# An MLP in two passes of half the tokens, its up projection by seven products of quarters

## The chip, the cores and the metric

The kernel runs on one core of a Trainium2 chip. The metric is the device time of one execution in microseconds (us). A core has TensorE for matrix products (PE in the profile), VectorE (DVE), ScalarE (ACT) and GpSimd (POOL) for the elementwise work, and DMA queues; SP is the engine that issues most DMAs, POOL issues the rest. Each engine takes its instructions in the order of its own program and waits on semaphores for the others. Matrix products go into PSUM, everything else lies in SBUF.

## The reference

The reference is one decoder layer on 1032 tokens (1024 of a prompt and 8 single steps of decoding), width 1024, with RMSNorm, one input projection, a pooling mixer and an RWKV-7 mixer, an output projection and an MLP. The change touches the last three lines:

```
mix = concatenate([pool_out, rwkv_out]) @ w_out
x = x + mix
h2 = rmsnorm(x, norm2_g)
x = x + square(relu(h2 @ w_up)) @ w_down        # w_up 1024x4096, w_down 4096x1024
y = rmsnorm(x, norm_f_g)
```

All of it is float32. The kernel splits each float32 operand into a high part h, rounded to the fp32r type, and a rest l, and computes a product as h·h + h·l + l·h: three matmuls.

## The kernel before

Features lie on the 128 partitions, tokens on the free axis: an activation of 1024 features is 8 tiles (index k or m), and the tokens are cut into blocks of 512, 260 and 260 columns (`BLK`). The residual x is held in two tiles, half 0 of 512 and half 1 of 520 tokens.

A weight tile is 128 x 512. `weights` (L147 to L167) loads it through POOL's queue into one of 4 buffers `wr`, ScalarE rounds it into `wh` (L92, the helper `act`) and VectorE subtracts, `wl` (L165); there are 6 pairs `wh`, `wl`. `gemm` (L169) issues the three matmuls for each of its input tiles (L175).

After the mixers comes the output projection (`mx`): first of half 0, then of half 1 (L938 to L949), where each of 8 m has two blocks of 21 matmuls of 260 columns. A block goes into one of two PSUM buffers (`ps_d`), and VectorE adds it to x (L880), which gives the buffer back. The x of half 1 comes by `load_x1` (L853). Then `norm2` makes h2 (h on ScalarE, l on VectorE, L913) and the root mean square.

The MLP: `up(f, w, b)` (L922) computes one of 32 feature tiles f for a token block: 24 matmuls (8 k times 3); VectorE applies relu and the scale (L931), squares (L932) and, after ScalarE's rounding, makes the rest `ul` (L934). `down(g, m, b, w)` takes four finished f (one g) for one m: 12 matmuls, and VectorE adds to x (L971). The loop L974 to L982 alternates four f of up with one g of down. Each weight is loaded once and serves the three blocks. The last g goes block by block with the final RMSNorm (L1001 to L1021), which VectorE applies (L993).

The order on each engine comes from a scheduler that takes the program text, buffers and dependencies and writes one list for each engine before the kernel runs; the buffers that a tile waits for are fixed with it.

## Time and profile before

| what | value |
| --- | --- |
| three runs | 1361.23, 1358.73, 1359.34 us; median 1359.34 |
| profiled execution | 1360.81 us, its span 1359.0 |
| mean granted clock of TensorE | 0.992 of full speed |
| TensorE busy | 1303.5 us, 96% of the span |
| VectorE busy | 823.5 us, 61% |
| ScalarE busy | 574.7 us, 42% |
| MLP, from first to last up and down product | about 614 to 1347 us |

Times below are from the profiled execution, in us from the start of its span, unless a duration is meant. A busy TensorE need not be at its peak: matmuls are pipelined, so the time that one costs is the distance from its start to the next one's, shorter than the duration shown. The same holds on VectorE. PEclk is the granted clock as a share of 2.4 GHz; 0.50 is 1.2 GHz.

### The profile page before, as it was taken

Reading aid. Unit: us, or ns where it says so; the run is one execution under the profiler, and the core shown is the slowest. Engines: PE = TensorE matmul, PEld = TensorE weight load, DVE = VectorE, ACT = ScalarE, POOL = GpSimd, SP = SyncE. Lnnn points to the kernel's source line nnn. Section 1 sums busy time; section 2 is a strip of 40 time slices with the busy share of each in tenths; the row PEclk is TensorE's granted clock in tenths of the full one; section 3 lists DMA queues with packets and bytes.
Section 4 is the critical chain, followed back from the end, with each engine's and each line's share of the span. In section 5 each row is a group of like instructions: output and inputs, shape, how many; then the busy total and the mean of one; then the engine's idle time right before and its main releaser. Section 6 shows DMA issues by size and latency. Waiting matters only on the chain.

```text
span 1359.0 us, 24513 instructions
## 1 busy us (share of the span) xinstructions
PE 1303.5 (96%) x9844; PEld 1154.2 (85%) x9844; DVE 823.5 (61%) x1790; ACT 574.7 (42%) x1417; POOL 156.9 (12%) x306
## 2 busy tenths in 40 slices
PE   5999999899999989899999999999999999999996
PEld 5987878798777867798999999999999999999986
DVE  7887686778777756749534435445344354453457
ACT  7668677766877666626211112112111121121123
POOL 4101001210100211120100000000000000000000
PEclk9999999999999979999999999999999999999998
DMA  6323123322211452621111111111111111111103
GB/s 204 102 54 80 42 49 90 102 87 61 62 51 40 105 175 100 201 92 47 56 51 44 50 47 45 49 46 47 50 46 48 47 46 47 46 48 49 47 6 125
DMA packets 81650, 94.55 MB, mean 70 GB/s; under 512 B 52504, under 2 KB 58776, under 8 KB 81528
## 3 DMA queue, kind: packets, MB, share of 16 engines
q0 software_dynamic: 20480, 66.04, 15.2%
q1 hardware_dynamic: 59728, 25.10, 7.2%
q8 instruction: 77, 1.26, 0.4%
q10 hardware_dynamic: 1328, 1.85, 0.4%
q14 instruction: 37, 0.30, 0.1%
HBM read 79.67 MB, written 13.51 MB: 69 GB/s over the span
## 4 chain that ended last, share of the span: by engine, by line
PE 78%; ACT 9%; DVE 7%; DMA 3%; issue 2%; POOL 0%; DVEq 0%; SPq 0%; ACTq 0%; POOLq 0%
PE dn L175 26%; PE up L175 26%; PE pj L175 8%; PE mx L175 5%; ACT SV L92 2%; PE pcs L598 1%; PE sc L421 1%; PE pcs L595 1%; ACT TT L92 1%; DVE tm L515 1%; PE pcs L591 1%; PE bkt L435 1%; DMA wr<-in_w_in 1%; PE py L599 1%; DMA x<-in_xT 1%
## 5 line engine op out<-in xcount | busy, mean ns | idle before, releaser
L92 ACT ACTIVATE wh<-wr 128x512 fp32r<-128x512 f32 x230 | 143.8, 626 | 355.7 <-PE dn L175 276.2
L175 PE MATMUL up<-h2h,wl 128*128 128x260 f32 (+1 forms) x768 | 245.6, 320 | 0.0
L175 PE MATMUL up<-h2h,wh 128*128 128x260 f32 (+1 forms) x768 | 245.0, 320 | 0.5 <-DVE u L931 0.5
L175 PE MATMUL up<-h2l,wh 128*128 128x260 f32 (+1 forms) x768 | 244.8, 319 | 0.0
L175 PE MATMUL dn<-uh,wl 128*128 128x512 f32 (+1 forms) x720 | 231.0, 321 | 0.0
L175 PE MATMUL dn<-ul,wh 128*128 128x512 f32 (+1 forms) x720 | 230.6, 320 | 0.0
L175 PE MATMUL dn<-uh,wh 128*128 128x512 f32 (+1 forms) x720 | 230.3, 320 | 0.0
L971 DVE TENSOR_TENSOR x<-dn,x 128x260 f32<-128x260 f32 (+1 forms) x192 | 99.1, 516 | 189.6 <-PE dn L175 189.6
L175 PE MATMUL pj<-xh,wh 128*128 128x258 f32 (+3 forms) x576 | 172.8, 300 | 13.9 <-ACT wh L92 13.9
L165 DVE TENSOR_TENSOR wl<-wr,wh 128x512 fp32r<-128x512 f32 x230 | 156.5, 684 | 44.7 <-ACT wh L92 38.0
L175 PE MATMUL pj<-xl,wh 128*128 128x258 f32 (+3 forms) x576 | 170.8, 297 | 0.0
L175 PE MATMUL pj<-xh,wl 128*128 128x258 f32 (+3 forms) x576 | 170.6, 296 | 0.1
L175 PEld LDWEIGHTS up<-h2l,wh 128*128 128x128 f32 x768 | 144.5, 188 | 12.1 <-DVE h2l L913 0.4
L175 PEld LDWEIGHTS up<-h2h,wh 128*128 128x128 f32 x768 | 144.1, 188 | 11.7 <-DVE u L931 0.9
L175 PEld LDWEIGHTS up<-h2h,wl 128*128 128x128 f32 x768 | 144.4, 188 | 11.1
L92 ACT ACTIVATE uh<-u 128x260 fp32r<-128x260 f32 (+1 forms) x96 | 47.2, 492 | 238.5 <-DVE u L932 238.5
L175 PEld LDWEIGHTS dn<-ul,wh 128*128 128x128 f32 x720 | 135.5, 188 | 10.9 <-issue 0.2
L175 PEld LDWEIGHTS dn<-uh,wh 128*128 128x128 f32 x720 | 135.7, 188 | 10.5
L175 PEld LDWEIGHTS dn<-uh,wl 128*128 128x128 f32 x720 | 135.4, 188 | 10.6 <-issue 0.2
L175 PEld LDWEIGHTS pj<-xh,wh 128*128 128x128 f32 x576 | 110.4, 192 | 17.8 <-ACT wh L92 13.9
L931 DVE SCALAR_TENSOR_TENSOR u<-up,rs 128x260 f32<-128x260 f32 (+1 forms) x96 | 49.5, 516 | 120.8 <-PE up L175 114.3
L175 PEld LDWEIGHTS pj<-xl,wh 128*128 128x128 f32 x576 | 110.6, 192 | 2.3 <-issue 1.9
(293 smaller groups left out, 2187.6 us busy)
## 6 DMA issues: line engine op xcount, KB each, us to landing
wr<-in_w_in POOLq DMA_DIRECT2D x72, 256.0 KB, 3.1
wr<-in_w_up POOLq DMA_DIRECT2D x64, 256.0 KB, 2.9
wr<-in_w_down POOLq DMA_DIRECT2D x64, 256.0 KB, 2.9
wr<-in_w_out POOLq DMA_DIRECT2D x26, 256.0 KB, 3.2
xr<-in_xT SPq DMA_DIRECT2D x16, 256.0 KB, 3.6
mr<-mix SPq DMA_DIRECT2D x8, 260.0 KB, 3.5
x<-in_xT SPq DMA_DIRECT2D x2, 1040.0 KB, 9.4
blk<-AA SPq DMA_DIRECT2D x16, 128.0 KB, 2.8
```

The source lines that it names most:

```text
L92: A.activation(out, in_, func, bias=bias, scale=scale, **k)
L165: V.tensor_tensor(l[:, :w], raw[:, :w], f32(h[:, :w]), op=ALU.subtract)
L175: PE.matmul(ps, lhs, rhs, start=i == 0, stop=i == n - 1)
L421: PE.matmul(psc[:, c, :], BK[:, c, 2 * h:2 * h + 2, :], AR[:, c, :, h, :], start=True, stop=True)
L435: PE.transpose(pt[:, c, :], BK[:, c, 2 * h:2 * h + 2, :].rearrange("p a t -> p (a t)"), ident)
L515: V.tensor_tensor(pr[:, q], l[:, q].unsqueeze(2).to_broadcast([64, m, m, m]), r[:, q].rearrange("p k j -> p j k").unsqueeze(1).to_broadcas ...
L591: PE.matmul(pq, AR[:, c, 0, :, :], SV[:, c, :, :], start=True, stop=True)
L595: PE.matmul(pa, TT[:, g, :, :], Q, start=True, stop=True)
L598: PE.matmul(pu, BKT[:, c, :, :], SV[:, c, :, :], start=True, stop=True)
L599: PE.matmul(py[:, c, :, :], SV[:, c, :, :], RB[:, c, :, :], start=False, stop=True)
L931: V.scalar_tensor_tensor(u, ps[:, :n], 0.0, rs2[:, cs], ALU.max, ALU.mult)
L971: V.tensor_tensor(d, ps[:, :n], d, op=ALU.add)
```

## The change

The tokens are processed in two passes: half 0 (512 tokens), then half 1 (520), and within a pass a product of a pair of feature tiles (256 output features), all 1024 inputs and the half's tokens is computed as a 2 x 2 by 2 x 2 block product by Strassen's scheme in Winograd's form. Quarters of the weights: output tile f or f+1 by inputs k 0 to 3 or 4 to 7. Quarters of the activations: inputs k 0 to 3 or 4 to 7 by the first or second half of the pass's tokens.

`up_operands(half)` normalises x fully and makes the seven activation operands (`KIND`), each as h and l, 4 tiles of 128 x 256 or 260. For each k of 4 it has 4 `normed`, 4 `less` and 7 `put`, so in all 60 instructions of VectorE and 28 of ScalarE for one half. `up_pair(p)` loads four weight quarters, single-buffered, through SP's queue, makes four sums on VectorE, splits seven operands, runs seven products of 12 matmuls of 256 or 260 columns, adds them up (`plus`, seven on VectorE) and applies relu and square on ScalarE (`emit`). Generators (`downs`) put down products of an earlier group between the products of a pair. Each weight of the MLP is now loaded twice, once for each half, which is 128 more loads of 256 KB, and all of them go through SP's queue. The final norm of half 0 comes in the middle (group 7), so the last group has only the two blocks of half 1.

```diff
+NXT = 8
+NUT = 10
...
-    def weights(src, into=None):
+    def weights(src, into=None, q=GP):
...
-                GP.dma_start(raw[:, :w], src[:, o:o + w])
+                q.dma_start(raw[:, :w], src[:, o:o + w])
...
+    def split(raw):
+
+        h = wp.tile([P, 512], F32R, tag="wh", name="wh", bufs=NWH)
+        l = wp.tile([P, 512], F32R, tag="wl", name="wl", bufs=NWH)
+        act(h, raw)
+        V.tensor_tensor(l, raw, f32(h), op=ALU.subtract)
+        return h, l
...
-    h2 = [hq.tile([P, KT, T], F32R, tag=f"h2{x}", name=f"h2{x}") for x in "hl"]
+
+    KIND = ("11", "t2", "21", "t3", "t1", "22", "t4")
+    XO = [{}, {}]
     rs2 = hq.tile([P, T], F32, name="rs2")
...
     def norm2(c, n, tmp):
-        for m in range(KT):
-            x, h, g = x1s(m, c, n), h2[0][:, m, c:c + n], col(V_G2, m)
-            act(h, x, scale=g)
-            V.scalar_tensor_tensor(h2[1][:, m, c:c + n], x, g, f32(h), ALU.mult, ALU.subtract)
         ss = ps_m.tile([P, 512], F32, tag="m", name=f"ss2{c}")
         acc = tmp(f"acc2{c}")[:, :n]
         for m in range(KT):
-            square_sum(ss, m, c, n, acc, m and tmp(f"sq2_{c}_{m}")[:, :n])
+            sq = tmp(f"sq2_{c}_{m}")[:, :n] if m else acc
+            act(sq, x1s(m, c, n), AF.Square)
+            if m:
+                V.tensor_tensor(acc, acc, sq, op=ALU.add)
+        PE.matmul(ss[:, :n], ON, acc, start=True, stop=True)
         rstd(rs2[:, c:c + n], ss[:, :n], tmp(f"ms2{c}")[:, :n], tmp(f"tt2{c}")[:, :n])
+    def up_operands(half):
+
+        c0, n = HALF[half]
+        q = n // 2
+        for i in KIND:
+            XO[half][i] = [hq.tile([P, 4, 260], F32R, tag=f"x{i}{x}", name=f"x{i}{x}{half}") for x in "hl"]
+
+        def put(i, k, x):
+            h, l = (t[:, k, :q] for t in XO[half][i])
+            act(h, x)
+            V.tensor_tensor(l, x, f32(h), op=ALU.subtract)
+
+        for k in range(4):
+            b = {}
+
+            def normed(i, kk, o):
+                b[i] = xtmp(f"b{i}_{k}_{half}", q)
+                V.scalar_tensor_tensor(b[i], x1s(kk, o, q), col(V_G2, kk), rs2[:, o:o + q], ALU.mult, ALU.mult)
+
+            def less(i, x, y, out):
+                V.tensor_tensor(b[out], b[x], b[y], op=ALU.subtract)
+                put(i, k, b[out])
+
+            normed("11", k, c0)
+            put("11", k, b["11"])
+            normed("21", k + 4, c0)
+            put("21", k, b["21"])
+            normed("12", k, c0 + q)
+            less("t1", "12", "11", "11")
+            normed("22", k + 4, c0 + q)
+            put("22", k, b["22"])
+            less("t2", "22", "11", "11")
+            less("t3", "22", "12", "12")
+            less("t4", "21", "11", "21")
+
     ups = {}
-    def up(f, w, b):
-        if f not in ups:
-            ups[f] = [mp.tile([P, T], F32R, tag=f"u{x}", name=f"u{x}{f}", bufs=6) for x in "hl"]
-        uh, ul = ups[f]
-        c, n = BLK[b]
-        cs = slice(c, c + n)
-        ps = ps_u.tile([P, 512], F32, tag="u", name=f"up{f}_{c}")
-        gemm(ps[:, :n], w, [(h2[0][:, k, cs], h2[1][:, k, cs]) for k in range(KT)])
-        u = tmp(f"u{f}_{c}")[:, :n]
-        V.scalar_tensor_tensor(u, ps[:, :n], 0.0, rs2[:, cs], ALU.max, ALU.mult)
-        V.tensor_tensor(u, u, u, op=ALU.mult)
-        act(uh[:, cs], u)
-        V.tensor_tensor(ul[:, cs], u, f32(uh[:, cs]), op=ALU.subtract)
+    def up_pair(p, between=()):
+
+        half, f0 = p // 16, 2 * (p % 16)
+        q = HALF[half][1] // 2
+        X = XO[half]
+        for f in (0, 1):
+            ups[2 * p + f] = [mp.tile([P, 520], F32R, tag=f"u{x}", name=f"u{x}{2 * p + f}", bufs=6) for x in "hl"]
+        a = {}
+        for k in range(2):
+            for f in range(2):
+                i = f"{f + 1}{k + 1}"
+                a[i] = mp.tile([P, 512], F32, tag=f"a{i}", name=f"a{i}_{p}")
+                SY.dma_start(a[i], I["w_up"][f0 + f][:, 512 * k:512 * k + 512])
+        for out, x, y, op in (("s3", "11", "21", ALU.subtract), ("s1", "21", "22", ALU.add), ("s2", "s1", "11", ALU.subtract),
+                              ("s4", "12", "s2", ALU.subtract)):
+            a[out] = mp.tile([P, 512], F32, tag=f"a{out}", name=f"a{out}_{p}")
+            V.tensor_tensor(a[out], a[x], a[y], op=op)
+        tmp = lambda x: mp.tile([P, 260], F32, tag="u", name=f"{x}_{p}", bufs=NUT)[:, :q]
+
+        banks = iter(range(7))
+
+        def product(s, x):
+            i = next(banks)
+            ps = (ps_u if i % 3 else ps_m).tile([P, 512], F32, tag="u" if i % 3 else "m", name=f"b{i}_{p}")[:, :q]
+            h, l = split(a[s])
+            for k in range(4):
+                c = slice(P * k, P * k + P)
+                xh, xl = (t[:, k, :q] for t in X[x])
+                for i, (lhs, rhs) in enumerate(((h, xh), (h, xl), (l, xh))):
+                    PE.matmul(ps, lhs[:, c], rhs, start=k == i == 0, stop=k == 3 and i == 2)
+            return ps
+
+        def emit(f, j, c):
+
+            cs = slice(j * q, j * q + q)
+            uh, ul = (t[:, cs] for t in ups[2 * p + f])
+            u = tmp(f"u{f}{j}")
+            act(c, c, AF.Relu)
+            act(u, c, AF.Square)
+            act(uh, u)
+            V.tensor_tensor(ul, u, f32(uh), op=ALU.subtract)
+
+        def plus(x, s, ps):
+            t = tmp(x)
+            V.tensor_tensor(t, s, ps, op=ALU.add)
+            return t
+
+        between = iter(between)
+        ps = product("11", "11")
+        p1 = tmp("p1")
+        act(p1, ps)
+        emit(0, 0, plus("c11", p1, product("12", "21")))
+        next(between, None)
+        u2 = plus("u2", p1, product("s2", "t2"))
+        next(between, None)
+        u3 = plus("u3", u2, product("s3", "t3"))
+        next(between, None)
+        ps = product("s1", "t1")
+        u4 = plus("u4", u2, ps)
+        emit(1, 1, plus("c22", u3, ps))
+        next(between, None)
+        emit(1, 0, plus("c21", u3, product("22", "t4")))
+        emit(0, 1, plus("c12", u4, product("s4", "22")))
     ps_u = open_pool(ctx, "psu", 4, space=PSUM)
     with tc.tile_pool(name="opb", bufs=1, reuse_waits="tile") as op:
         ops = [mixed(op, k, 1, 3) for k in range(KT - 1)]
         load_x1(1)
+        norm2(0, 512, lambda x: op.tile([P, 512], F32, tag="n2", name=x, bufs=2))
+        up_operands(0)
         for m in range(KT):
             w = weights(I["w_out"][m, :, :(KT - 1) * P])
             for o in (0, 260):
                 out_block(m, w, ops, 1, o, 260)
-        norm2(0, 512, lambda x: op.tile([P, 512], F32, tag="n2", name=x, bufs=2))
...
+    def down(g, m, blk, w):
+        c, n = blk
+        half = int(c > 0)
+        o = c - 512 * half
+        ps = ps_d.tile([P, 512], F32, tag="d", name=f"dn{g}_{m}_{c}")
+        gemm(ps[:, :n], w, [tuple(t[:, o:o + n] for t in ups[32 * half + 4 * g + j]) for j in range(4)])
         d = x1s(m, c, n)
         V.tensor_tensor(d, ps[:, :n], d, op=ALU.add)
-    for f in range(1, 4):
-        ups_of(f)
-    for g in range(7):
-        ups_of(4 * g + 4)
-        for m in range(KT):
-            w = weights(I["w_down"][g, m])
-            for b in range(3):
-                down(g, m, b, w)
-        for f in range(4 * g + 5, 4 * g + 8):
-            ups_of(f)
-
-
...
+    up_pair(0)
+    for c, n in BLK[1:]:
+        norm2(c, n, tmp)
+    up_pair(1)
+    def downs(G, ms):
+        half, g = G // 8, G % 8
+        for m in ms:
+            w = weights(I["w_down"][g, m], q=SY)
+            for blk in MB[half]:
+                down(g, m, blk, w)
+            yield
+
+    for G in range(15):
+        first, rest = downs(G, range(4)), downs(G, range(4, 8))
+        if G == 7:
+            up_operands(1)
+            for _ in first:
+                pass
+        up_pair(2 * G + 2, rest if G == 7 else first)
+        up_pair(2 * G + 3, () if G == 7 else rest)
+        if G == 7:
+            for c in (0, 256):
+                ss = ps_m.tile([P, 512], F32, tag="m", name=f"ss30{c}")[:, :256]
+                acc = tmp(f"acc30{c}", "acc")[:, :256]
+                for m in range(KT):
+                    sq = tmp(f"sq3_{c}_{m}")[:, :256] if m else acc
+                    act(sq, x1s(m, c, 256), AF.Square)
+                    if m:
+                        V.tensor_tensor(acc, acc, sq, op=ALU.add)
+                PE.matmul(ss, ON, acc, start=True, stop=True)
+                for x in final_scale((c, 256), ss):
+                    final(*x)
+
+
...
+    ws = [weights(I["w_down"][7, m], None if m < 4 else w7[m - 4], q=SY) for m in range(KT)]
+    pending = []
+    for b in (1, 2):
+        c, n = BLK[b]
...
```

In the change, line numbers move: L880 of before is L890, L165 is L167, L971 is L1054.

**Output projection of half 1, VectorE.** `mx1_m_o` is the block of output tile m at column o; x11 is the residual of half 1. Before, the additions stand close together:

```order
L880 TENSOR_TENSOR x11_7047<-mx1_0_0_7_7122,x11_7047 128x260
L880 TENSOR_TENSOR x11_7047<-mx1_0_260_7_7145,x11_7047 128x260
L165 TENSOR_TENSOR wl_7293<-wr_7290,wh_7292 128x384
L904 TENSOR_TENSOR acc20_7591<-acc20_7591,sq2_0_6_7608 128x512
L904 TENSOR_TENSOR acc20_7591<-acc20_7591,sq2_0_7_7611 128x512
L880 TENSOR_TENSOR x11_7047<-mx1_1_0_7_7180,x11_7047 128x260
L165 TENSOR_TENSOR wl_7345<-wr_7342,wh_7344 128x512
L880 TENSOR_TENSOR x11_7047<-mx1_1_260_7_7203,x11_7047 128x260
```

With the change the addition of `mx1_1_260` stands behind the operands of half 0 (`b..`, `x..l0`, `xt..l0`); 51 rows of that kind are left out here:

```order
L890 TENSOR_TENSOR x11_7047<-mx1_1_0_7_7329,x11_7047 128x260
L942 SCALAR_TENSOR_TENSOR b11_0_0_7155<-x10_6510,vec_87,rs2_7057 128x256
L942 SCALAR_TENSOR_TENSOR b21_0_0_7159<-x10_6510,vec_87,rs2_7057 128x256
...
L945 TENSOR_TENSOR b12_3_0_7241<-b22_3_0_7246,b12_3_0_7241 128x256
L935 TENSOR_TENSOR xt1l0_7150<-b11_3_0_7233,xt1h0_7149 128x256
L890 TENSOR_TENSOR x11_7047<-mx1_1_260_7_7352,x11_7047 128x260
L945 TENSOR_TENSOR b11_3_0_7233<-b22_3_0_7246,b11_3_0_7233 128x256
L935 TENSOR_TENSOR xt3l0_7148<-b12_3_0_7241,xt3h0_7147 128x256
```

Between the additions of `mx1_1_0` and `mx1_1_260` stood one weight split; now there are 55 instructions (16 of L942, 39 of L935 and L945). The matmuls of `mx1_2_260` need the PSUM buffer that the second addition gives back.

**First weights of the MLP.** Before, they are on POOL's queue behind those of the output projection, and wait for a `wr` buffer and the queue alone:

```order
L157 DMA wr_7522<-in_w_out 128x384 [waits DMASW2_49,DVE_49]
L155 DMA wr_7629<-in_w_out 128x4x128 [waits DMASW3_49,DVE_49]
L155 DMA wr_7635<-in_w_out 128x4x128 [waits DMASW4_49,DVE_49]
L157 DMA wr_7725<-in_w_up 128x512 [waits DMASW5_49,DVE_49]
L157 DMA wr_7731<-in_w_up 128x512 [waits DMASW6_49,DVE_49]
L157 DMA wr_7927<-in_w_up 128x512 [waits DMASW7_49,DVE_49]
```

With the change they are on SP's queue, in tiles `a` of the MLP's own pool, which is opened after the pool `opb` of the output projection is closed:

```order
L866 DMA x11_7047<-in_xT 128x4x520
L159 DMA wr_8304<-in_w_down 128x512 [waits DMASW5_49,DMASW1_49,DMASW6_49,DMASW0_49,DVE_49]
L159 DMA wr_8343<-in_w_down 128x512 [waits DMASW2_49,DMASW6_49,DMASW0_49,DVE_49]
L159 DMA wr_8382<-in_w_down 128x512 [waits DMASW7_49,DMASW3_49,DVE_49]
L159 DMA wr_8428<-in_w_down 128x512 [waits DMASW4_49,DMAHW3_49,DMASW0_49,DVE_49]
L974 DMA a11_0_7829<-in_w_up 128x512 [waits DMAHW4_49,PE_49]
L974 DMA a21_0_7831<-in_w_up 128x512 [waits DMAHW5_49]
L974 DMA a12_0_7833<-in_w_up 128x512 [waits DMAHW6_49]
L974 DMA a22_0_7835<-in_w_up 128x512 [waits DMAHW7_49]
```

The first of them, `a11_0`, waits for TensorE: for the last matmul of the output projection. The first split on VectorE (`wl` from `a11_0`) is its row 1037, the first addition of a down product (`dn0_0`) its row 1122; the additions and splits of three pairs and some operands of half 1 stand between them. Before, the first addition of a down product follows rows of the up products alone.

**From half 0 to half 1, VectorE.** Before, there is no such place, and rows of up and down follow each other:

```order
L971 TENSOR_TENSOR x11_7047<-dn0_6_2_8665,x11_7047 128x260
L165 TENSOR_TENSOR wl_8938<-wr_8935,wh_8937 128x512
L971 TENSOR_TENSOR x10_6510<-dn0_7_0_8685,x10_6510 128x512
L971 TENSOR_TENSOR x11_7047<-dn0_7_1_8699,x11_7047 128x260
L971 TENSOR_TENSOR x11_7047<-dn0_7_2_8713,x11_7047 128x260
L165 TENSOR_TENSOR wl_8944<-wr_8941,wh_8943 128x512
L931 SCALAR_TENSOR_TENSOR u5_0_8766<-up5_0_8741,rs2_7059 128x512
L932 TENSOR_TENSOR u5_0_8766<-u5_0_8766 128x512
```

With the change, 31 rows stand between the last `plus` of pair 15 and the next down weights, 28 of them of `up_operands(1)` (the last four are shown), and behind them the weight splits for the next down products (`wl_119..`) and the sums and splits of pair 16:

```order
L945 TENSOR_TENSOR b21_3_1_11907<-b21_3_1_11907,b11_3_1_11903 128x260
L935 TENSOR_TENSOR xt2l1_11814<-b11_3_1_11903,xt2h1_11813 128x260
L935 TENSOR_TENSOR xt3l1_11818<-b12_3_1_11911,xt3h1_11817 128x260
L935 TENSOR_TENSOR xt4l1_11824<-b21_3_1_11907,xt4h1_11823 128x260
L167 TENSOR_TENSOR wl_11952<-wr_11949,wh_11951 128x512
L167 TENSOR_TENSOR wl_11972<-wr_11969,wh_11971 128x512
L167 TENSOR_TENSOR wl_11992<-wr_11989,wh_11991 128x512
L978 TENSOR_TENSOR as2_16_12025<-as1_16_12023,a11_16_12013 128x512
L176 TENSOR_TENSOR wl_12031<-a11_16_12013,wh_12030 128x512
L978 TENSOR_TENSOR as4_16_12027<-a12_16_12017,as2_16_12025 128x512
L1054 TENSOR_TENSOR x10_6510<-dn7_1_0_11955,x10_6510 128x512
```

TensorE's list has `dn7_0`, `dn7_1`, `dn7_2` and the first matmuls of pair 16 there: 20 matmuls stand before the first that needs `wl_11952`. Behind pair 16 comes pair 17, which has no down products in between, while VectorE has the final norm of half 0.

## Rows read from the trace of the kernel before

**Rows 1.** page, busy time by engine

```profile
PE 1303.5 (96%) x9844; PEld 1154.2 (85%) x9844; DVE 823.5 (61%) x1790; ACT 574.7 (42%) x1417; POOL 156.9 (12%) x306
```

**Rows 2.** windows: stretches of 40, 25 and 100 us, with column names

```profile
core 0: us, PE busy (x) PEld busy (x) DVE busy (x) ACT busy (x) POOL busy (x), PEclk, DMA share, GB/s
560.00:600.00 40.00, 36.45 (x278) 34.80 (x277) 22.04 (x41) 15.07 (x27) 7.44 (x13) 1.00 0.52 171
625.00:650.00 25.00, 23.74 (x145) 20.50 (x144) 22.08 (x51) 13.10 (x30) 3.22 (x6) 1.00 0.19 60
700.00:800.00 100.00, 100.00 (x640) 90.74 (x639) 44.97 (x83) 16.67 (x29) 9.67 (x18) 1.00 0.15 48
```

**Rows 3.** chain that ended last: start us, us, engine, work

```profile
565.74 8.38 DMA x<-in_xT
574.63 35.41 PE mx L175 x294
721.53 45.20 PE up L175 x288
766.73 45.31 PE dn L175 x288
1353.36 2.40 DVE x L993 x6
```

**Rows 4.** timeline of TensorE, matmuls of 512, 260 and 256 columns: start, us

```profile
721.83 0.39 PE L175 MATMUL up<-h2h,wl 128*128 128x512 f32 x1
726.94 0.28 PE L175 MATMUL up<-h2h,wh 128*128 128x260 f32 x1
732.55 0.28 PE L175 MATMUL up<-h2h,wl 128*128 128x260 f32 x1
...
42.05 0.28 PE L175 MATMUL pj<-xh,wh 128*128 128x256 f32 x1
44.77 0.28 PE L175 MATMUL pj<-xh,wl 128*128 128x256 f32 x1
```

**Rows 5.** timeline of VectorE: instructions back to back

```profile
539.58 0.68 DVE L165 TENSOR_TENSOR wl<-wr,wh 128x512 fp32r<-128x512 f32 x1
541.38 0.68 DVE L691 TENSOR_TENSOR dS<-dS,dT 128x512 f32<-128x512 f32 x1
542.10 0.69 DVE L693 TENSOR_TENSOR dS<-dS,dW 128x512 f32<-128x512 f32 x1
...
615.73 0.76 DVE L880 TENSOR_TENSOR x<-mx,x 128x260 f32<-128x260 f32 x2
629.33 1.28 DVE L913 SCALAR_TENSOR_TENSOR h2l<-x,vec,h2h 128x260 fp32r<-128x260 f32 x3
```

**Rows 6.** timeline of VectorE, out projection of half 1

```profile
574.14 0.77 DVE L880 TENSOR_TENSOR x<-mx,x 128x260 f32<-128x260 f32 x2 [0.87 <-DMA x<-in_xT]
577.46 0.43 DVE L880 TENSOR_TENSOR x<-mx,x 128x260 f32<-128x260 f32 x1
```

**Rows 7.** waits of TensorE: engine line <- releaser: us, times, longest

```profile
PE po L773 <- DMA pw<-in_pool_w: 3.4, 1, 3.4
PE mx L175 <- DVE x L880: 2.9, 1, 2.9
```

**Rows 8.** windows about 478 us; columns as in rows 2

```profile
478.00:480.00 2.00, 0.00 (x0) 0.00 (x0) 0.00 (x0) 1.57 (x4) 0.00 (x0) 0.50 1.02 393
483.00:484.00 1.00, 1.00 (x4) 0.48 (x2) 0.96 (x3) 0.00 (x0) 0.00 (x1) 0.50 0.20 61
484.00:485.00 1.00, 1.00 (x34) 0.73 (x33) 0.47 (x1) 0.00 (x0) 0.00 (x0) 0.83 0.02 4
```

**Rows 9.** lines of 640 to 1298 us by shape: VectorE's and ScalarE's halves of the split

```profile
L165 DVE TENSOR_TENSOR wl<-wr,wh 128x512 fp32r<-128x512 f32 x116 | 80.1, 690 | 14.5 <-ACT wh L92 12.1
L92 ACT ACTIVATE wh<-wr 128x512 fp32r<-128x512 f32 x116 | 73.5, 633 | 300.7 <-PE dn L175 276.2 <-PE up L175 24.2
```

**Rows 10.** page, DMA issues: KB each, us from issue to landing

```profile
wr<-in_w_up POOLq DMA_DIRECT2D x64, 256.0 KB, 2.9
```

More of the change, by code (lines that the diff above doesn't have):

```diff
@@ L154, in weights @@
             if len(src.shape) > 2:
[L155 removed]
+                q.dma_start(raw.rearrange("p (m c) -> p m c", c=P), src)
             else:
[L157 removed]
+                q.dma_start(raw[:, :w], src[:, o:o + w])
             if into:
@@ L997, in final, with final_scale @@
             (A if m == 3 else SY).dma_start(O["yT"][:, m + 1 - k:m + 1, c:c + n], x1[h][:, m + 1 - k:m + 1, o:o + n])
-    for b, (c, n) in enumerate(BLK):
+    def final_scale(blk, ss):
+        c, n = blk
+        rs = mp.tile([P, 260], F32, tag="rs3", name=f"rs3{c}", bufs=2)[:, :n]
+        rstd(rs, ss[:, :n], tmp(f"ms3{c}")[:, :n], tmp(f"tt3{c}")[:, :n])
+        return [(blk, m, rs) for m in range(KT)]
+    up_pair(0)
[29 more added lines that the diff above has]
+                    final(*x)
+    w7 = [[hq.tile([P, 4, 260], F32R, tag=f"x{i}{x}", name=f"w7{i}{x}").rearrange("p k t -> p (k t)")[:, :512]
+           for x in "hl"] for i in KIND[:4]]
+    ws = [weights(I["w_down"][7, m], None if m < 4 else w7[m - 4], q=SY) for m in range(KT)]
+    pending = []
+    for b in (1, 2):
+        c, n = BLK[b]
         ss = ps_u.tile([P, 512], F32, tag="u", name=f"ss3{b}")
@@ L1002, in _build @@
         for m in range(KT):
-            down(7, m, b, ws[m])
+            down(7, m, BLK[b], ws[m])
             d = x1s(m, c, n)
@@ L1016, in _build @@
             pending = []
-        rs = mp.tile([P, 512], F32, tag="rs3", name=f"rs3{b}", bufs=2)[:, :n]
-        rstd(rs, ss[:, :n], tmp(f"ms3{b}")[:, :n], tmp(f"tt3{b}")[:, :n])
-        pending += [(b, m, rs) for m in range(KT)]
+        pending += final_scale(BLK[b], ss)
     for q in pending:
```

36 lines of the change are left out of this document (7 added, 29 removed).

## Prediction

> **What bounds the kernel now.** I read the busy shares first: TensorE 96% of the span, VectorE 61%, ScalarE 42% [rows 1]. That average hides stages, so the windows came next: in 700 to 800 us TensorE is busy all of the time, VectorE 45 and ScalarE 17 of 100 us, the clock is full and the DMA engines are used to 15% [rows 2]. The reader should see that nothing but TensorE's matmuls sets the pace there. The chain of waits says the same: one stretch of 288 up matmuls, one of 288 down matmuls, 45.2 and 45.3 us, and nothing between [rows 3]. Before the MLP it is different: the chain runs through the load of x (lands at 574.1) and then 294 matmuls of the output projection [rows 3].
>
> What a matmul costs is its pitch. From 721.83 to 726.94 are 22 steps of 512 columns, 0.232 us each; from 726.94 to 732.55 are 47 steps of 260 columns, 0.119; from 42.05 to 44.77 are 23 steps of 256, 0.118 [rows 4]. So 256 columns cost about half of 512, and a product cut into smaller blocks loses nothing on TensorE.
>
> VectorE's instructions overlap a little too: 512 columns start 0.60 us apart (539.58 to 541.38, three steps) though each lasts 0.68; where one reads what the one ahead of it wrote the step is 0.72 (541.38 to 542.10). For 260 columns two take 0.76, so the step is 0.345; with a pointer scalar three take 1.28, so 0.40 [rows 5].
>
> **The change part by part.** *Up products.* Before: 32 f of 72 matmuls, that is eight stretches of 288 and 8 x 45.2 = 361.6 us. After: 32 pairs of 84 matmuls, 1344 of 256 columns and 1344 of 260: 1344 x 0.118 + 1344 x 0.119 = 319. Gain 42.5. The down products keep their 2304 matmuls in the same shapes, 0.
>
> *Steady pairs.* A pair with four m of down products costs TensorE 84 x 0.118 + 48 x 0.232 = 21.0 us in half 0 and 84 x 0.119 + 96 x 0.119 = 21.5 in half 1. VectorE has for it four sums, seven splits and four weight splits of 512 columns, seven `plus` and four `emit` of 256, and the additions (four of 512 or eight of 260): 15 x 0.60 + 11 x 0.345 + 2.4 or 2.8 = 15.2 to 15.6 us, 73% instead of 45%. ScalarE stays under it. Each pair also needs eight loads of 256 KB, 2 MB in 21 us, 100 GB/s, where the load of one takes 2.9 us [rows 10] and 393 GB/s have been moved at once [rows 8]. So TensorE hides them, if no single wait in order sticks out. I take 1 us in all, from below 0 (excluded: TensorE is already 100% busy there) to 8, a quarter us for each pair.
>
> *Output projection of half 1, place (a).* VectorE's list has 55 instructions between the additions of the second and the third block pair, and `mx1_2_260` needs the PSUM buffer that the later addition frees. In the trace the first two additions stand at 574.14, the third at 577.46 [rows 6]; with the norm's three instructions I put the third at 578. Then 16 x 0.40 + 39 x 0.345 = 19.9 us, and the addition of `mx1_1_260` ends at 578 + 0.35 + 19.9 = 598.3. TensorE resumed at 574.63 [rows 3] and has three blocks of 21 matmuls to do, 3 x 21 x 0.119 = 7.5, till 582.1. It waits 16.2 us. The clock: about 478 us TensorE waited 3.4 us for a load [rows 7], the granted clock was 0.50 in 478 to 480, still 0.50 (1.2 GHz) in 483 to 484 and 0.83 in the next microsecond [rows 8], so about 4.5 us after the resume ran at half pace, which costs 2.3. After a wait of 2.9 us [rows 7] the clock stayed at 1.00 [rows 2]. A wait of 16 us is on the former side: (a) = 18.5. Bounds: 15, all at 0.345, an earlier start and no drop; 21, waits for ScalarE's roundings among the 55. These 20 us of VectorE stood elsewhere before, as h2's rows, but there TensorE lost only 1.3 us (23.74 of 25) [rows 2], which goes: -1.3.
>
> *Start of the MLP, place (b).* The first weight quarter is loaded only after the last matmul of the output projection. Then 2.9 us of load, 0.63 of rounding, 0.69 of subtraction [rows 9, 10]: TensorE idles 4 us. Behind it VectorE's rows 1037 to 1117 stand ahead of what the first down product needs: 36 of 512, 40 of 256 or 260 and 5 with a pointer, 36 x 0.605 + 40 x 0.345 + 5 x 0.40 = 37.6 us, from 3.5 us after the last matmul on, and some 2 us of waits for the later quarters: at 43 the last operand is there, at 44 `dn0_0` is done. TensorE's list up to it has 208 matmuls of 256 columns and 19 of 512, 208 x 0.118 + 19 x 0.232 = 29.0. Behind VectorE by 15; with 1 for the clock, which matters little while TensorE waits anyway, (b) = 16. Before, weights were preloaded on another queue, and the comparable cost is in the 1.3 above. Bounds: 12 (VectorE at its shortest steps, waits hidden), 21 (each quarter's wait shows and the clock comes late).
>
> *Between the halves, place (c).* After the last product of pair 15 VectorE has one `plus`, 31 rows of 11.2 us (25 x 0.345 + 5 x 0.40 + 0.60) and the split that `dn7_1` needs: 0.35 + 11.2 + 0.69 = 12.2. TensorE has 16 matmuls of 512 and 4 of 260 in the meantime, 4.2 us. It waits 8.0; 2.3 more for the clock; then pair 17 has no down products (10.0 us of TensorE) while VectorE has its 13 us for the pair and, for half 0's final norm, 16 x 0.40 + 14 x 0.345 = 11.2 us more. Some of this lies under pair 16 and 18: I take 3 of at most 14. (c) = 13.3; bounds 8 and 20.
>
> *Tail.* The last down block, the norm and the last eight scalings (through 1353.36 and on) are the same [rows 3]: 0.
>
> **Sum.** -42.5 + 18.5 + 16 + 13.3 - 1.3 + 1 = +5.0. Against the profiled execution, 1360.8: 1365.8. This was 1.5 above the median of the three runs, 1359.3, so I expect 1364 for the median. By the lower ends it is -42.5 + 15 + 12 + 8 - 1.3 = -8.8, or 1350.5; by the upper ones -42.5 + 21 + 21 + 20 - 1.3 + 8 = +26.2, or 1385.5. All three at one end at once is unlikely.
>
> **Rivals.** *The saving shows (faster).* TensorE is the only bound, and the three places cost only their lower ends because VectorE reaches them ahead of its list's worst case: 1350.5. For it: in the trace VectorE has 55% of the time free [rows 2] and adds to blocks at once [rows 6]. Against it: order, not load, decides, and the lists are fixed. It decides against my forecast from a sum of the three below 38.5, that is 9 less than I have.
>
> *Every VectorE instruction costs its whole duration.* Then 0.085 us more for each: 55 x 0.085 = 4.7 at (a), 81 x 0.085 = 6.9 at (b), 38 x 0.085 = 3.2 at (c): +14.8, 1379. For it only the dependent pair at 541.38 [rows 5]; against it the three steps of 0.60 before. The Trainium skill, page VectorE: DVE Perf Modes, section "The DRAIN you can't avoid", has this as a rule: the next op does not start until the pipe is empty, after every op. The trace does not agree where nothing depends: 0.60 from start to start at a duration of 0.68.
>
> *Steady pairs wait.* The quarters are single-buffered: the next pair's load of `a22` starts only when its split and sums have read it, and VectorE in order holds all behind a sum that waits for a load of 2.9 us. If 1 us of it reaches TensorE in each of 30 pairs: +30, 1394. For it: 73% of VectorE in order; against: six pairs of `wh`, `wl`, about 8 us of TensorE's work ahead.
>
> *The matmuls don't get fewer in time.* Columns fall from 792,576 to 693,504 in the up products, or the pitch would have to rise: excluded by 0.118 at 256 columns [rows 4].
>
> **How the numbers follow.** A median within 0.2%, 2.7 us, of 1359.3 can't be told from no change. Chances: my forecast 0.55, with its own range 1356 to 1374; the faster rival 0.25; full VectorE durations 0.10; waiting pairs 0.10. Of the forecast's 0.55, 0.20 lies within 2.7 us of before and 0.35 above. So faster 0.25, same 0.20, slower 0.35 + 0.10 + 0.10 = 0.55. The range 1349 to 1380 takes in the faster rival, the forecast and full durations, and leaves out the waiting pairs and a stray 10%.
>
> **What would show it.** In the profile after: TensorE busy about 42 us less; in the waits of TensorE, one of about 16 us for VectorE's addition in the output projection (near 582), with 0.50 granted after it; the first MLP matmul some 4 us after the last of the output projection, and a loss of 15 us till `dn0_0`; a wait of 8 us near the middle of the MLP; from there windows with TensorE at 100%, VectorE near 73%. I am wrong if the wait at 582 is under 10 us, if the pairs of the steady state last over 22 us, or if 12 up matmuls of 256 columns take more than 1.45 us.

## The result and the profile after

The changed kernel took 1368.41 us (median of five runs, 1364.55 to 1369.36), the kernel before 1360.16 (five runs, 1358.73 to 1361.58): 1.0057 times as long, 95% interval 1.0039 to 1.0075. The forecast was 1364 us and slower. The profiled execution has a span of 1367.6 us, 8.6 more than before.

The page first: busy time by engine, to be held against [rows 1].

```profile
PE 1277.1 (93%) x10228; PEld 1156.3 (85%) x10228; DVE 1060.8 (78%) x2321; ACT 827.3 (60%) x2004; POOL 88.1 (6%) x178
```

TensorE was busy 26.4 us less (1303.5 to 1277.1) and idle 35.0 us more (55.5 to 90.5): that is the 8.6. By the forecast the products alone should have taken 42.5 us off its busy time; the missing 16 us went into matmuls at half clock, for the mean granted clock fell from 0.992 to 0.979. As an estimate from these means, the busy time counted at full clock falls from 1303.5 x 0.992 to 1277.1 x 0.979, by 42.8 us. So the saving came, and more than that was paid back, in waits and in the clock behind them.

Windows of the profile after, columns as in [rows 2]: the out projection of half 1 and the start of the MLP (two windows each), the steady pairs of half 0, the middle, the steady pairs of half 1.

```profile
575.00:600.00 25.00, 9.38 (x65) 9.17 (x65) 23.77 (x66) 12.37 (x31) 0.00 (x0) 0.70 0.03 11
600.00:625.00 25.00, 25.00 (x199) 25.00 (x199) 8.59 (x18) 4.51 (x8) 3.66 (x6) 0.94 0.34 101
640.00:660.00 20.00, 16.39 (x107) 15.51 (x108) 18.71 (x40) 14.65 (x35) 0.00 (x0) 0.85 0.33 109
660.00:680.00 20.00, 16.17 (x98) 15.01 (x97) 16.07 (x35) 10.63 (x25) 0.00 (x0) 0.81 0.28 79
700.00:800.00 100.00, 100.00 (x618) 89.55 (x617) 77.14 (x143) 53.95 (x110) 0.00 (x0) 1.00 0.34 103
975.00:1000.00 25.00, 18.80 (x83) 15.07 (x83) 21.46 (x47) 11.20 (x26) 0.00 (x0) 0.80 0.26 85
1100.00:1200.00 100.00, 100.00 (x837) 100.00 (x836) 80.15 (x159) 52.89 (x107) 0.00 (x0) 1.00 0.33 101
```

In the steady stretches TensorE is busy all of the time at full clock, with VectorE at 77 and 80 of 100 us; nearly all losses lie in 575 to 680 and about 975, and some 2.5 us more in small waits between 1030 and 1090. The chain that ended last shows the length of a steady pair: start, duration and work, where [rows 3] had the long stretches of up and down products.

```profile
883.73 5.68 PE b L991 x48
904.77 5.68 PE b L991 x48
...
1242.28 5.76 PE b L991 x48
1263.83 5.75 PE b L991 x48
```

From one to the next are 21.04 us in half 0 and 21.55 in half 1; 21.0 and 21.5 were worked out. The waits of TensorE by what released them (total, times, longest), against [rows 7]:

```profile
PE mx L185 <- DVE x L890: 18.2, 6, 15.6
PE b L991 <- ACT wh L94: 5.8, 4, 3.2
PE dn L185 <- DVE x L1054: 5.4, 3, 4.1
PE ss L922 <- DVE acc L921: 3.2, 1, 3.2
PE b L991 <- DVE wl L176: 2.8, 3, 2.3
PE dn L185 <- DVE wl L167: 2.1, 1, 2.1
```

The first row is the out projection of half 1. VectorE's timeline shows how the 15.6 us come about (the rows of before are [rows 6]):

```profile
576.37 0.43 DVE L890 TENSOR_TENSOR x<-mx,x 128x260 f32<-128x260 f32 x1 [0.95 <-PE mx L185]
576.71 1.66 DVE L942 SCALAR_TENSOR_TENSOR b<-x,vec,rs 128x256 f32<-128x256 f32 x4
...
579.00 0.42 DVE L935 TENSOR_TENSOR x21l<-b,x21h 128x256 fp32r<-128x256 f32 x1
579.34 0.42 DVE L945 TENSOR_TENSOR b<-b,b 128x256 f32<-128x256 f32 x1
579.68 0.43 DVE L935 TENSOR_TENSOR x22l<-b,x22h 128x256 fp32r<-128x256 f32 x1
...
596.52 0.41 DVE L890 TENSOR_TENSOR x<-mx,x 128x260 f32<-128x260 f32 x1
```

TensorE's next matmul, in its own timeline:

```profile
596.99 0.58 PE L185 MATMUL mx<-mh,wh 128*128 128x260 f32 x1 [15.62 <-DVE x L890]
```

The addition of the block at 576.37 is followed at once by the operands of half 0, 55 instructions with a single gap of 0.28 us, and the next addition is at 596.52; TensorE, which has waited 15.62 us for it, goes on at 596.99.

Three durations sum it up, all from the timelines: from TensorE's resume behind the load of x to its last out projection matmul, 64.4 us (572.02 to 636.46); from there to the first addition of a down product, 48.7 (685.15); from there to the last down matmul, 670.4 (1355.60). They go from start to start.

### The profile page after: what moved, and what is told of

Read it like the earlier page. It is cut to its first block, busy times and chain, and to the rows that moved or that the text cites. A ratio compares the mean times of both kernels' runs of the same rounds, so it can differ in the third digit from the quotient of the medians.

```text
span 1367.6 us, 26992 instructions
## 1 busy us (share of the span) xinstructions
PE 1277.1 (93%) x10228; PEld 1156.3 (85%) x10228; DVE 1060.8 (78%) x2321; ACT 827.3 (60%) x2004; POOL 88.1 (6%) x178
## 4 chain that ended last, share of the span: by engine, by line
PE 72%; DVE 12%; ACT 10%; DMA 3%; issue 2%; POOL 1%; SPq 0%; DVEq 0%; ACTq 0%; POOLq 0%
PE dn L185 24%; PE b L991 21%; PE pj L185 10%; PE mx L185 6%; ACT SV L94 2%; PE pcs L608 1%; DVE tm L525 1%; PE sc L431 1%; PE pcs L605 1%; ACT TT L94 1%; PE pcs L601 1%; ACT wh L94 1%; DVE x L1060 1%; DMA a<-in_w_up 1%; PE bkt L445 1%
## 5 line engine op out<-in xcount | busy, mean ns | idle before, releaser
L185 PE MATMUL dn<-uh,wh 128*128 128x260 f32 (+1 forms) x736 | 237.8, 324 | 6.0 <-DVE x L1054 5.4
L185 PE MATMUL dn<-uh,wl 128*128 128x260 f32 (+1 forms) x736 | 237.5, 323 | 2.1 <-DVE wl L167 2.1
L185 PE MATMUL dn<-ul,wh 128*128 128x260 f32 (+1 forms) x736 | 237.3, 323 | 0.1
L167 DVE TENSOR_TENSOR wl<-wr,wh 128x512 fp32r<-128x512 f32 x230 | 156.0, 682 | 31.6 <-ACT wh L94 22.5
L1054 DVE TENSOR_TENSOR x<-dn,x 128x260 f32<-128x260 f32 (+1 forms) x192 | 98.7, 514 | 68.0 <-PE dn L185 64.8
L94 ACT ACTIVATE wh<-as 128x512 fp32r<-128x512 f32 x128 | 80.1, 628 | 76.5 <-PE dn L185 72.7
L94 ACT ACTIVATE wh<-a 128x512 fp32r<-128x512 f32 x96 | 60.5, 632 | 104.1 <-PE dn L185 56.0
L185 PEld LDWEIGHTS pj<-xh,wl 128*128 128x128 f32 x576 | 110.1, 191 | 1.8 <-issue 1.0
L176 DVE TENSOR_TENSOR wl<-as,wh 128x512 fp32r<-128x512 f32 x128 | 87.9, 687 | 4.6
L185 PE MATMUL mx<-mh,wh 128*128 128x260 f32 (+1 forms) x192 | 67.2, 352 | 18.6 <-DVE x L890 18.2
L1002 DVE TENSOR_TENSOR ul<-u,uh 128x256 fp32r<-128x256 f32 (+1 forms) x128 | 54.1, 425 | 21.7 <-ACT uh L94 21.5
L176 DVE TENSOR_TENSOR wl<-a,wh 128x512 fp32r<-128x512 f32 x96 | 65.8, 687 | 4.9 <-ACT wh L94 1.0
```

The costliest lines, as they stand in the source:

```text
L94: A.activation(out, in_, func, bias=bias, scale=scale, **k)
L167: V.tensor_tensor(l[:, :w], raw[:, :w], f32(h[:, :w]), op=ALU.subtract)
L176: V.tensor_tensor(l, raw, f32(h), op=ALU.subtract)
L185: PE.matmul(ps, lhs, rhs, start=i == 0, stop=i == n - 1)
L1002: V.tensor_tensor(ul, u, f32(uh), op=ALU.subtract)
L1054: V.tensor_tensor(d, ps[:, :n], d, op=ALU.add)
```

## The experiments

The theory: TensorE loses time only at three places, and at each because an instruction that it needs stands behind others in the order of one engine's list. The rivals: VectorE's load as such (78% of the span) takes the time, wherever its instructions stand; or VectorE costs TensorE time in the steady pairs too. Ratios below are to the kernel before, run on the same chip, with their 95% intervals; the change itself is 1.0057. As the runs stand on several chips, a difference from the change is that of the two ratios, times 1360 us; against e6 it is that of the medians, unless said.

**e1: operands of half 0 spread over the out projection.** `up_operands` becomes a generator that yields behind each operand.

```diff
-        up_operands(0)
+        parts = up_operands(0)
         for m in range(KT):
             w = weights(I["w_out"][m, :, :(KT - 1) * P])
             for o in (0, 260):
                 out_block(m, w, ops, 1, o, 260)
+                if m:
+                    next(parts, None), next(parts, None)
+        for _ in parts:
+            pass
```

> Edit: the 60 VectorE instructions of up_operands(0) are put into the program text in portions of one or two operands between the blocks of the output projection of half 1, instead of all ahead of them. Nothing is left out. Theory (order: an addition that frees a PSUM buffer stands behind 55 instructions): the 15.6 us wait at 596.99 and the half clock behind it go, about -18 us, so about 1350 us against 1368; VectorE has the same number of instructions. Rival (load: VectorE's work has only been moved and is late elsewhere): the saving comes back as longer waits in the start of the MLP, less than 5 us are left, 1364 or more.

Measured: 1349.9 us, ratio 0.9922 (0.9906 to 0.9939), 18.4 us less than the change. The wait of 15.6 us is gone; of TensorE's waits for an addition this is left (15.6 was the longest), while VectorE is busy for 1060.2 us as in the change, 1060.8:

```profile
PE mx L185 <- DVE x L890: 2.1, 5, 1.5
```

The 1.5 us are the wait behind the load of x, which the change has too (1.9).

From the resume to the last out projection matmul are 44.4 us instead of 64.4, and the stretch behind it is as long as it was (48.8 against 48.7). So nothing came back later: order, not load. The rival falls.

**e2: quarters of the first pair loaded early.**

```diff
-                a[i] = mp.tile([P, 512], F32, tag=f"a{i}", name=f"a{i}_{p}")
+                a[i] = hq.tile([P, 512], F32, tag=f"a{i}", name=f"a{i}_{p}")
```

> Edit: the four weight quarters a are taken from the pool that is open since before the output projection, so the loads of pair 0 need not wait for its last matmul. Nothing is left out. Theory: the 3.2 us from the last matmul of the output projection to the first of the MLP go, and VectorE makes the first splits and sums (about 8 us of its list) earlier, so -5 to -9 us: about 1361 us against 1368. Rival (half 1's norm, not the load, sets the start of the MLP): only the 3 us at most, and the wait for the sum of squares grows by as much: 1367 or more.

Measured: 1376.33 us, ratio 1.0122 (1.0104 to 1.0141): 9 us slower than the change (8 by the medians). The theory missed; the rival's "1367 or more" takes in the number, but its reason does not hold: the wait for the sum of squares is shorter (1.2 us for 3.2), not longer. The 3.2 us wait at the first product went (one of 2.5 us came at a later product), but TensorE waits 7.0 us for the roundings `mh` of the mixer's output (three times, 3.3 at most) in the out projection.

**e3: down products ahead of the operands of half 1.**

```diff
         if G == 7:
-            up_operands(1)
             for _ in first:
                 pass
+            up_operands(1)
```

> Edit: between the halves the first four down products of group 7 stand in the program text ahead of up_operands(1) instead of behind it. Nothing is left out. Theory (order): TensorE has 11 us of down products while VectorE makes the operands; the waits of 4.1 and 2.1 us and the half clock go, -8 us: about 1360 us against 1368. Rival (VectorE has 17 us of work there in any order): TensorE waits as long, only later, for the first product of pair 16: 1366 or more.

Measured: 1363.53 us, ratio 1.0016 (1.0003 to 1.0029), 5.6 less than the change. The waits of 4.1 and 2.1 us are gone, and one of 2.4 us for the first product of the operands (at 986.14, with half clock behind it) has come: between the two expectations (1360, and 1366 or more). From the first down addition to the last down matmul, the stretch that the edit touches, e3 takes 665.4 us, 5.1 less than the change.

**e4: norm of half 1 later.**

```diff
     up_pair(0)
-    for c, n in BLK[1:]:
-        norm2(c, n, tmp)
     up_pair(1)
...
         up_pair(2 * G + 3, () if G == 7 else rest)
+        if G == 1:
+            for c, n in BLK[1:]:
+                norm2(c, n, tmp)
```

> Edit: the sums of squares and the norm of the two blocks of half 1 come after group 1's pairs instead of between pair 0 and pair 1. Nothing is left out. Theory (VectorE's list sets the start of the MLP): 25 instructions fewer stand ahead of the first down addition, 25 x 0.345 = 8.6 us, and the wait of 3.2 us for the sum of squares goes: -8 us, about 1360 us against 1368. Rival (the late first load alone sets the start): no more than the 3.2 us of that wait: 1365 or more.

Measured: 1357.78 us, ratio 0.9979 (0.9968 to 0.9990), 10.6 less than the change. The first addition of a down product comes 35.0 us after the last out projection matmul instead of 48.7:

```profile
672.30 0.68 DVE L1054 TENSOR_TENSOR x<-dn,x 128x512 f32<-128x512 f32 x1
```

This is the row on VectorE; in the change the same one stands at 685.15. The rival (1365 or more) falls. The stretch is 13.7 us shorter, more than the 8.6 of the instructions moved: the wait for the sum of squares (3.2 us) and two falls of the clock went with them. Behind it 3.4 us come back: the norm now stands there, and from the first down addition to the last down matmul are 673.8 us instead of 670.4.

**e5: early quarters, on POOL's queue.** As e2, with the loads of `a` issued by GpSimd, to see if e2 lost by SP's queue.

```diff
-                SY.dma_start(a[i], I["w_up"][f0 + f][:, 512 * k:512 * k + 512])
+                GP.dma_start(a[i], I["w_up"][f0 + f][:, 512 * k:512 * k + 512])
```

> Edit: as in e2 the four weight quarters come from the pool that is open early, but their loads stand on POOL's queue, behind the weights of the output projection, and no longer on SP's. Nothing is left out. Theory (e2 lost because on SP's queue the early loads moved the load of x ahead of loads of the mixer's output): those waits of TensorE (7.0 us in e2) are away and the 3.2 us wait at the start of the MLP goes: 1360 to 1365 us. Rival (early splits and sums themselves disturb the output projection): still 1372 or more.

Measured: 1378.85 us, ratio 1.0133 (1.0116 to 1.0151), no better than e2: SP's queue was not it. The number is the rival's (1372 or more), but its cause, the early work itself, is not borne out by e10 below, at least for two of the quarters. ScalarE's timeline shows what differs. First the change, the first square of half 0's norm and the first two roundings of the mixer's output:

```profile
552.58 0.62 ACT L94 ACTIVATE acc<-x 128x512 f32<-128x512 f32 x1
555.54 1.29 ACT L94 ACTIVATE mh<-mr 128x520 fp32r<-128x520 f32 x2
```

Then e5, the same instructions with the weight rounding ahead of them:

```profile
563.42 0.52 ACT L94 ACTIVATE wh<-wr 128x384 fp32r<-128x384 f32 x1 [2.16 <-PE mx L185]
563.85 0.61 ACT L94 ACTIVATE acc<-x 128x512 f32<-128x512 f32 x1
566.27 1.15 ACT L94 ACTIVATE mh<-mr 128x520 fp32r<-128x520 f32 x2
```

They come 11 us later, because four roundings of out projection weights now stand ahead of them in ScalarE's list, and each of these waits for matmuls to give a weight buffer back. The edit makes the early pool larger by 8 KB for each partition; that this is why the scheduler changes these rows is argued, not shown. e10, which keeps the pool's size, has the first rounding `mh` at 559.10, where e6, with the same orders elsewhere, has 559.88.

**e6: e1, e3 and e4 together.**

> Edit: e1, e3 and e4 together (operands of half 0 spread over the output projection, down products of group 7 ahead of the operands of half 1, norm of half 1 after group 1). Nothing is left out. Theory (three separate places, each set by the order on VectorE): the three savings add up, 18.4 + 5.6 + 10.6 = 35 us, about 1334 us against 1368 and 1360 of before. Rival (VectorE's load is the limit, the savings come out of the same 78% busy engine): less than 25 us in all, 1344 or more.

Measured: 1339.79 us, ratio 0.9841 (0.9826 to 0.9857): 29 us less than the change, 22 less than the kernel before. The rival (1344 or more) falls. The out projection lasts 44.5 us and the start of the MLP 35.4, as in e1 and e4 alone. The savings don't add up in full: some 6 of 35 us are missing. In the traces 2.2 of them lie behind the first down addition: from there to the last down matmul e6 takes 671.0 us, where the change with the differences of e3 (-5.1) and e4 (+3.4) would take 668.8. Another 2.6 were never the edits': in e3 and e4 the out projection is 1.4 and 1.3 us shorter than in the change, though neither edit touches it, for the clock did not fall behind the load of x there.

**e7: e6 and e5 together.**

> Edit: e6 and e5 together. Nothing is left out. Theory: 3 to 8 us less than e6, as the first load no longer waits for the output projection. Rival (VectorE's splits and sums set the start of the MLP once the norm is away): within 2 us of e6.

Measured: 1348.05 us, ratio 0.9901 (0.9884 to 0.9917), 8 us slower than e6. Neither expectation held: as in e5, TensorE waits 6.0 us for `mh` in the out projection.

**e8: eight products for seven, in the order of e6.** `KIND` is then the four plain quarters; the sums, differences and `plus` are left out, and two products at a time run on in one PSUM tile. VectorE has 14 instructions fewer in each pair:

```diff
-    KIND = ("11", "t2", "21", "t3", "t1", "22", "t4")
+    KIND = ("11", "21", "12", "22")
...
+            for kk in range(2):
+                h, l = w[f, kk]
+                for k in range(4):
+                    c = slice(P * k, P * k + P)
+                    xh, xl = (t[:, k, :q] for t in X[f"{kk + 1}{j + 1}"])
+                    for i, (lhs, rhs) in enumerate(((h, xh), (h, xl), (l, xh))):
+                        PE.matmul(ps, lhs[:, c], rhs, start=kk == k == i == 0, stop=kk == 1 and k == 3 and i == 2)
```

> Edit: e6 with the 2 x 2 blocks multiplied out plainly: eight products of quarters, accumulated in pairs in PSUM, no sums of weights or activations and no plus. Same outputs; 384 more matmuls of 256 or 260 columns, 15 instead of 26 or so VectorE instructions for each pair. Theory (in the steady pairs TensorE alone sets the time): 384 x 0.119 = 45.6 us more, less some 5 us in the start and the middle where VectorE's list is shorter: e6 + 36 to + 46. Rival (VectorE at 73 to 78% costs TensorE time in the steady pairs too): much less, e6 + 25 or under.

Measured: 1367.24 us, ratio 1.0047 (1.0031 to 1.0063), e6 + 27.4: between the two. The pages of e6 and e8 (busy time by engine) tell why:

```profile
PE 1273.4 (95%) x10228; PEld 1154.0 (86%) x10228; DVE 1058.0 (79%) x2321; ACT 826.0 (62%) x2004; POOL 88.4 (7%) x178
```

```profile
PE 1306.1 (96%) x10612; PEld 1189.6 (87%) x10612; DVE 824.9 (60%) x1817; ACT 748.8 (55%) x1852; POOL 88.1 (6%) x178
```

TensorE is busy 32.7 us longer in e8, not 45.6, for e6 has more matmuls at half clock (mean 0.985 against 0.993, some 10 us); and e8 idles 7 us less. In the steady stretches both have TensorE at 100%, and by the timelines a steady pair lasts 22.4 to 22.5 us in half 0 and 22.8 to 23.0 in half 1, where e6 has 21.0 to 21.1 and 21.55 to 21.59: 1.4 us for each of 32 pairs. So the seven products bring their 45 us there, and e6 gives 18 of it back. Some 5 of these are chance, ahead of all edits: in 500 to 540 us the clock is 0.91 in e6 and 1.00 in e8, and e8 resumes behind the load of x at 571.04, e6 at 575.73. From there to the last down matmul e8 takes 30.6 us longer (781.5 for 750.9), so about 15 are given back in waits and half clock at the start and the middle. Two passes with eight products are no gain: they cost 6 us against the kernel before.

**e9: every sum of weight quarters made twice, in the order of e6.**

```diff
             V.tensor_tensor(a[out], a[x], a[y], op=op)
+            V.tensor_tensor(a[out], a[x], a[y], op=op)
```

> Edit: e6 with each of the four sums of weight quarters made twice by VectorE (128 more instructions of 128x512, about 77 to 90 us of VectorE). Same outputs. Theory (in the steady pairs TensorE alone sets the time, VectorE has 27% to spare): a steady pair lasts 21.0 and 21.5 us as before, VectorE near 85 of 100 us in the windows there, and only the start and the middle, where VectorE's list decides, get longer: e6 + 4 to + 12, 1344 to 1352 us. Rival (VectorE at 78% already costs TensorE time in the pairs): each pair longer by 1 us or more, e6 + 35 or more.

Measured: 1351.8 us, ratio 0.9930 (0.9917 to 0.9944), e6 + 12. The windows of e6 and then of e9 in the steady pairs of both halves:

```profile
700.00:900.00 200.00, 200.00 (x1246) 179.56 (x1245) 160.53 (x303) 112.97 (x237) 0.00 (x0) 1.00 0.35 102
1100.00:1300.00 200.00, 200.00 (x1672) 200.00 (x1671) 158.49 (x314) 109.58 (x224) 0.00 (x0) 1.00 0.33 94
```

```profile
700.00:900.00 200.00, 200.00 (x1252) 179.66 (x1251) 178.93 (x339) 110.61 (x234) 0.00 (x0) 1.00 0.33 100
1100.00:1300.00 200.00, 200.00 (x1671) 200.00 (x1671) 173.37 (x349) 106.07 (x218) 0.00 (x0) 1.00 0.31 93
```

VectorE goes from 80 to 89 of 100 us in half 0 and from 79 to 87 in half 1, and TensorE stays at 100%; the steady pairs are 21.0 to 21.1 us apart in half 0 and 21.55 to 21.59 in half 1, as in e6. All of the loss lies in the start (the first down addition 42.5 us after the out projection instead of 35.4) and the middle. The rival falls: load does no harm up to 89% where nothing waits in order.

**e10: two quarters early, places kept.** e6 with `a11` and `a21` in the early pool and half as many temporaries.

```diff
-NXT = 8
+NXT = 4
...
+                a[i] = (hq if k == 0 else mp).tile([P, 512], F32, tag=f"a{i}", name=f"a{i}_{p}")
```

> Edit: e6 with two of the four weight quarters (a11, a21) taken from the pool that is open early, and 4 instead of 8 buffers for the temporaries of the operands, so that the pools behind keep their places and ScalarE's roundings of the mixer's output their rows. Nothing is left out. Theory (e2 and e5 lost by the moved rows of ScalarE, not by the early load): no wait for those roundings, the wait of 3.3 us at the first product goes, and as the other two quarters still come late the gain is small: e6 - 1 to - 4. Rival (an early load of the quarters itself costs time): e6 + 5 or more, as e2 and e5 lost 8 and 10.

Measured: 1338.65 us, ratio 0.9839 (0.9826 to 0.9853): 1.1 us less than e6, and 0.3 by the ratios, so no difference that can be told from none. TensorE waits 0.9 us for `mh` where e2 and e5 had 7.0 and 6.0, so the early load as such does no harm, and the rival falls; but the 3.35 us wait only moved to the product of the first quarter that comes late. What all four in time would give stays open.

**e11: norm of half 0 after group 9, in the order of e6.**

```diff
-        if G == 7:
+        if G == 9:
             for c in (0, 256):
```

> Edit: e6 with the final norm of half 0 (30 VectorE, 16 ScalarE instructions) after group 9 instead of group 7. Nothing is left out. Theory (behind the change of halves VectorE has the norm on top of two pairs of which one has no down products): the waits of 1.0 and about 1.2 us between 1000 and 1050 us go, and nothing appears later since a steady pair has room for it: e6 - 2 to - 5. Rival (those waits come from the pair without down products alone): within 1 us of e6.

Measured: 1336.08 us, ratio 0.9822 (0.9808 to 0.9835), 3.7 less than e6 by the medians, 2.6 by the ratios (the two stand on different chips, and the intervals overlap), and the lowest of all. The window of 1000 to 1050 us in e6, then in e11:

```profile
1000.00:1050.00 50.00, 47.71 (x388) 46.73 (x387) 45.39 (x102) 29.73 (x64) 0.00 (x0) 1.00 0.44 132
```

```profile
1000.00:1050.00 50.00, 50.00 (x419) 50.00 (x419) 40.03 (x79) 25.14 (x52) 0.00 (x0) 1.00 0.33 101
```

TensorE waits no longer there. But two waits of nearly the same length stand where the norm now is:

```profile
1087.44 0.39 PE L185 MATMUL dn<-uh,wh 128*128 128x260 f32 x1 [0.82 <-DVE x L1065]
1104.60 0.39 PE L998 MATMUL b<-xt2h,wh 128*128 128x260 f32 x1 [1.02 <-ACT wh L94]
```

So the waits go with the norm, and "nothing appears later" did not hold. Of the 4.1 us between the spans of the two traces, 2.4 stand ahead of the edit (resume behind the load of x at 573.31 for 575.73) and 1.5 behind the first down addition (669.5 for 671.0): what the edit is worth is about 1.5 us by the traces, less than the medians differ, and not clear of the noise.

## Why the prediction was right, and where its sizes were off

*Products and steady pairs.* Right. (The sum's own terms give a gain of 361.6 - 318.5 = 43.1 us, not 42.5.) Pair lengths are as worked out and e8 shows the price of the eighth product, e9 the room that VectorE has. Its share was put too low, 73% where 77 and 80 are busy; the number of instructions is as counted (30 and 34 for each pair), so it is their price that was low: the sum has them all at the step of instructions back to back. Two rivals fall: steady pairs don't wait, and VectorE's instructions don't cost their full durations where they stand close: the 55 at place (a) take 19.8 us (576.71 to 596.52), 19.9 were worked out. In the fence of place (a) above, the starts at 579.00, 579.34 and 579.68 are 0.34 us apart at a duration of 0.42, as 0.345 was taken. The Trainium skill (page VectorE: DVE Perf Modes, section "The DRAIN you can't avoid") gives as a rule that the next op waits until the pipe is empty, which these rows do not bear out; but the same paragraph adds that "A next op that is not held starts earlier", held being its word for an instruction that must wait for all earlier ones. The rows agree with that, and the rival of the prediction took the rule without it.

*Place (a).* Forecast 18.5. The wait is 15.62 us, worked out as 16.2; the stretch of the out projection is 20.0 us longer than in e1 by the traces, and e1 saves 18.4 by the ratios. Where the traces have 1.5 more, the clock fell once more than assumed: it stood near half in 572 to 574 already, behind a wait of 1.9 us (last fence below). In e1 it did not fall there.

*Place (b).* This term was mis-sized: forecast 16, found 48.7 - 29.0 = 19.7 (29.0 is the prediction's sum for TensorE's list). VectorE's list was counted nearly right: from its first split, 3.4 us behind the last matmul, to the addition it has 85 instructions and works 39.9 us, where 81 and 37.6 were taken; the addition was put at 44 us and found at 48.7. What was too small is the allowance for VectorE's own waits: 2 us were allowed, and it idles 5.3. The longest three are:

```profile
661.77 0.43 DVE L921 TENSOR_TENSOR acc<-acc,sq 128x260 f32<-128x260 f32 x1 [1.14 <-ACT sq L94]
671.02 0.43 DVE L137 TENSOR_TENSOR tt<-rs 128x260 f32<-128x260 f32 x1 [1.34 <-ACT rs L94]
675.18 0.69 DVE L167 TENSOR_TENSOR wl<-wr,wh 128x512 fp32r<-128x512 f32 x1 [0.94 <-ACT wh L94]
```

The last two hang on TensorE: ScalarE's `rs` comes behind the matmul that ends the sum of squares, and its `wh` waits for products to give a weight buffer back. So "1 for the clock, which matters little while TensorE waits anyway" was too little as well. TensorE did not wait once: it waited 3.2 us (to 639.90), 2.3 (to 656.56) and 3.2 (to 668.34), and behind each the clock fell to 0.50 to 0.59:

```profile
640.00:642.00 2.00, 1.78 (x8) 1.57 (x9) 1.52 (x3) 0.77 (x3) 0.00 (x0) 0.59 0.52 165
642.00:644.00 2.00, 2.00 (x12) 2.00 (x11) 1.95 (x4) 0.99 (x4) 0.00 (x0) 0.55 0.00 0
...
656.00:658.00 2.00, 1.44 (x10) 1.44 (x11) 2.00 (x5) 2.00 (x6) 0.00 (x0) 0.86 0.43 151
658.00:660.00 2.00, 2.00 (x11) 2.00 (x11) 2.00 (x6) 1.57 (x4) 0.00 (x0) 0.50 0.29 112
...
668.00:670.00 2.00, 1.66 (x5) 1.47 (x6) 1.68 (x4) 0.39 (x1) 0.00 (x0) 0.50 0.82 252
672.00:674.00 2.00, 2.00 (x11) 2.00 (x11) 1.96 (x5) 0.86 (x2) 0.00 (x0) 0.50 0.00 0
```

These windows are the change's, columns as in [rows 2]. So VectorE's list waited for matmuls at half clock in its turn; how much of the 5.3 us the clock made, no run shows apart. The third wait, for the sum of squares of half 1's norm, was not named: it stands in TensorE's list ahead of products that don't need it. e4 takes it away: VectorE then works 29.6 us and idles 1.8 till the addition.

*Place (c).* Forecast 13.3 and 1 for the pairs; from the first down addition on, what is left of the sum is about 15, a remainder and not a measurement. One wait of 8.0 us for a split was worked out; the trace has two, 4.1 for an addition and 2.1 for a split, 6.2 in all, both behind the operands of half 1 as expected, with half clock behind them. Two more of 1.0 us come with the norm of half 0: in e11 they move with it.

*The sum.* From the resume behind the load of x to the last down matmul the change takes 11.0 us longer (772.6 to 783.6) where +5.0 was forecast: 1.5 at (a), 3.7 at (b), about 1 behind it. In the profiled executions the stages ahead were 2.6 us quicker (resume at 572.02 for 574.63); the experiments without waits for `mh` have it between 571 and 576, so that is no part of the change, and that it brings the measured time nearer to the forecast is luck. So the sign and mechanism were right, and the clock at (a) and VectorE's waits at (b) were under-priced.

*The rival on the faster side* did not come true. e1 comes to its time (1349.9 us for 1350.5), but by another order, and not because VectorE reaches the three places early.
